# Dropping semaphore waits that another wait implies, in a row-wise absolute maximum

## The chip, the cores and the metric

The kernel runs on one core of one Trainium2 chip. The metric is the device time of one execution in microseconds (us), measured outside the profiler; a profile's "span" leaves out some 2.7 us of it. Executions that are compared ran on the same chip in the same rounds.

## The reference

```python
def setup_inputs():
    return {"x": np.random.randn(8192, 8192).astype(np.float32)}

def reference(x):
    return np.linalg.norm(x, ord=np.inf, axis=1)
```

For a matrix, this norm with `axis=1` is the largest absolute value of each row: 268 MB are read and 32 KB written.

## The kernel before

SyncE (SP) issues every load, and VectorE (DVE) reduces each loaded buffer. There are three buffers of 128 x 16384 numbers in turn (8.4 MB each). Twenty-four bulk loads fill whole buffers; the rest of the matrix comes in pieces that get smaller, so that little is left to reduce when the last piece lands.

```python
    sbuf = ctx.enter_context(tc.tile_pool(name="sbuf", bufs=BUFS))     # BUFS = 3
    ...
    def absmax(o, i):
        return nc.vector.reduce_max(out=o, in_=i, axis=X, apply_absolute_value=True)

    for a in range(A):
        for n in range(G):
            t = sbuf.tile([P, W + PAD], F32, tag="t")
            nc.sync.dma_start(out=t[:, :W], in_=x_b[a, n])             # 24 bulk loads
            absmax(r_bulk[:, a, n * B : (n + 1) * B], ...)
    for i, loads in enumerate(TAIL):                                   # 7 tiles, 21 loads
        ...
    # the last tile: 13 loads, each reduced as it lands, then the last store
    nc.sync.dma_start(out=out_t, in_=r_tail[:])
```

A load into a used buffer has two reasons to wait. The buffer's previous load must have landed (a semaphore of one of eight "lanes", raised by the DMA engines), and the reduction of that data must be over (one counter, raised by VectorE). As this program is built, a load or a reduction carries at most one wait itself; its other waits stand in wait-only instructions (`EVENT_SEMAPHORE` in the profile) ahead of it, one or two in each. As built, a bulk load is this pair:

```text
SP EventSemaphore  waits lane 0 >= 16        the earlier load of this buffer has landed
SP DMACopy         waits DVE    >= 2         its reduction is over; then issue
```

The first wait says nothing new: the reduction itself waited for that landing.

## Time and profile before

| quantity | value | from |
|---|---|---|
| time | 627.62 us median of 6 (627.34 to 628.16) | runs beside the changed kernel |
| span | 624.7 us | page |
| rate in the bulk | 434 GB/s, 19.33 us a load | windows |
| issue to landing of a bulk load | 40.7 us median | line of the load |
| one bulk reduction | 17.22 us | groups |
| fetches of instructions during the span | 2, of 8 KB each | queue 14 |

Two lines of the view of SyncE's waits show what the prediction rests on (who waits, for whom: us in total, times, longest us).

```profile
SPq L187 <- DVE r_bulk L180: 361.6, 21, 17.2
SPq L187 <- DMA t<-in_x_dram: 54.8, 21, 20.1
```

SyncE waits twice for each of the 21 bulk loads, and the wait for VectorE is the one that ends last, after 17.2 us.

```profile
q14 instruction: 2, 0.02, 0.0%
```

### The profile page before, as it was taken

The page shows a single profiled execution, that of the slowest core. Times are in us where ns is not written, and L with a number is a line of the kernel's source. Part 1 is how long each engine was busy: PE and PEld are TensorE (multiplying, and loading weights), DVE is VectorE, ACT ScalarE, POOL GpSimd, SP SyncE. Part 2 cuts the span into 40 slices and gives each one's busy share as a digit, 9 for nine tenths or more (in the row PEclk, how much of TensorE's full clock was granted, in tenths as well). Part 3 has the DMA queues.
Part 4 walks back from the last instruction along what each step waited for, and adds up shares of the span by engine and source line. Part 5 has one row for each costly group of instructions (what it writes and reads, how often), then busy time and mean ns, then how long its engine had stood idle before and what let it go on. Part 6 is the DMA issues. An engine that isn't in the chain of part 4 may idle for free.

```text
span 624.7 us, 189 instructions
## 1 busy us (share of the span) xinstructions
DVE 553.0 (89%) x67; POOL 0.2 (0%) x4
## 2 busy tenths in 40 slices
DVE  0588988889988889888898888988889999999999
POOL 0000000000000000000000000000000000000000
DMA  9999999999999999999999999999999999999998
GB/s 403 462 411 453 420 449 424 432 441 403 470 403 470 403 470 403 453 420 453 420 441 432 424 449 403 470 403 470 403 438 425 445 417 443 421 427 432 423 423 342
DMA packets 9138, 268.48 MB, mean 430 GB/s; under 512 B 1712, under 2 KB 1712, under 8 KB 3248
## 3 DMA queue, kind: packets, MB, share of 16 engines
q1 hardware_dynamic: 8352, 268.44, 99.6%
q10 hardware_dynamic: 784, 0.02, 0.1%
q14 instruction: 2, 0.02, 0.0%
HBM read 268.44 MB, written 0.03 MB: 430 GB/s over the span
## 4 chain that ended last, share of the span: by engine, by line
DMA 67%; DVE 31%; issue 1%; another core or an unknown queue 0%; DVEq 0%; SPq 0%
DMA t<-in_x_dram 67%; DVE r_bulk L180 24%; DVE part L180 6%; DVE t L180 2%; DVEq L270 0%; DVE r_tail L180 0%; SPq L199 0%
## 5 line engine op out<-in xcount | busy, mean ns | idle before, releaser
L180 DVE TENSOR_REDUCE r_bulk<-t 128x2 f32<-128x16384 f32 x24 | 413.3, 17220 | 69.7 <-DMA t<-in_x_dram 69.7
L180 DVE TENSOR_REDUCE part<-t 128x1 f32<-128x8192 f32 (+20 forms) x28 | 121.5, 4411 | 0.3 <-DMA t<-in_x_dram 0.3
L180 DVE TENSOR_REDUCE t<-t 128x1 f32<-128x1664 f32 (+8 forms) x11 | 16.7, 1577 | 0.1
L180 DVE TENSOR_REDUCE r_tail<-t 128x1 f32<-128x644 f32 (+1 forms) x2 | 1.6, 818 | 0.0
L177 DVE MEMSET part<- 128x56 f32 x1 | 0.1, 105 | 0.9 <-PEq L259 0.9
L180 DVE TENSOR_REDUCE r_tail<-part 128x14 f32<-128x56 f32 x1 | 0.2, 202 | 0.0
L259 POOL MEMSET const-bfloat16-1.0<- 128x1 bf16 x1 | 0.1, 103 | 0.0
L259 POOL MEMSET const-uint8-127<- 128x1 uint8 x1 | 0.1, 102 | 0.0
L259 POOL MEMSET const-float32-0.0<- 128x1 f32 x1 | 0.1, 100 | 0.2 <-issue 0.2
L259 POOL MEMSET const-float32-1.0<- 128x1 f32 x1 | 0.1, 99 | 0.0
## 6 DMA issues: line engine op xcount, KB each, us to landing
t<-in_x_dram SPq DMA_DIRECT2D x2, 3392.0 KB, 37.2
t<-in_x_dram SPq DMA_DIRECT2D x1, 5376.0 KB, 40.5
t<-in_x_dram SPq DMA_DIRECT2D x1, 4864.0 KB, 32.9
t<-in_x_dram SPq DMA_DIRECT2D x1, 4800.0 KB, 32.8
t<-in_x_dram SPq DMA_DIRECT2D x1, 4672.0 KB, 34.7
t<-in_x_dram SPq DMA_DIRECT2D x3, 1536.0 KB, 36.9
t<-in_x_dram SPq DMA_DIRECT2D x1, 3520.0 KB, 42.7
t<-in_x_dram SPq DMA_DIRECT2D x1, 3328.0 KB, 40.4
```

The source lines that it names most:

```text
L177: nc.vector.memset(part[:], 0.0)
L180: return nc.vector.reduce_max(out=o, in_=i, axis=X, apply_absolute_value=True)
L259: nc = _bacc.Bacc("TRN2", target_bir_lowering=False, num_devices=1)
```

## The change

When the program is finalized, a pass walks through it. It notes which lane values VectorE must have seen by each value of its counter. A lane wait of a load or store on SyncE is dropped where the VectorE value that the same instruction waits for implies it. On VectorE, a wait for its own counter is dropped where the load whose landing is waited for was itself issued behind that value. Twenty-nine wait-only instructions on SyncE and two on VectorE disappear; nothing is added or reordered. The core of the diff:

```diff
+def drop_implied_waits(nc):
+    ...
+        if type(i).__name__ == "InstDMACopy":
+            ...
+            if i.engine == sp and own and len(waits) > 1:
+                known = upto[own - 1]
+                insts[n] = rewait(i, [s for s in waits
+                    if s.id == counter or s.wait_value > known.get(s.id, 0)])
+        elif i.engine == dve and own and len(waits) > 1:
+            past = max(behind.get((s.id, s.wait_value), 0) for s in waits)
+            if past >= own:
+                insts[n] = rewait(i, [s for s in waits if s.id != counter])
     ...
+    nc.at_finalize(drop_implied_waits)
     nc.at_finalize(start_first_load_early)
```

(Lines are joined here; cuts are marked with dots.)

## The prediction

> **What bounds the kernel now.** I read the page first (busy shares, slices, queues), then the windows, then the order of time in the stream and at the end. The page of the kernel before says that the transfers are never idle; VectorE (DVE) is the only computing engine that does anything to speak of:
>
> ```profile
> span 624.7 us, 189 instructions
> DVE 553.0 (89%) x67; POOL 0.2 (0%) x4
> DMA  9999999999999999999999999999999999999998
> DMA packets 9138, 268.48 MB, mean 430 GB/s; under 512 B 1712, under 2 KB 1712, under 8 KB 3248
> ```
>
> The reader is to see the row of nines: there is no slice in which the 16 DMA engines stand still. The view by windows gives the rate in a stretch of the bulk, in which three loads of 8.389 MB (128 partitions x 16384 numbers of 4 bytes) pass, and in the last part (columns: window, its length, DVE busy, POOL busy, clock, DMA share, GB/s):
>
> ```profile
> 136.00:194.00 58.00, 51.66 (x3) 0.00 (x0) 1.00 1.00 434
> 600.00:612.00 12.00, 11.99 (x7) 0.00 (x0) 1.00 1.01 424
> ```
>
> Three loads in 58.00 us are 19.33 us a load. One bulk reduction takes 17.22 us, so DVE waits about 2.1 us for each load; in the last 150 us it works without a gap, level with the transfers. 268.44 MB at 434 GB/s are 618.5 us. About 6.2 us of the 624.7 us span are the start, the slightly slower small loads and the finish. So the kernel is bound by transfer rate, and a removed instruction can help only where it makes a transfer start earlier into an empty queue, or shortens the last few microseconds.
>
> How full is the queue? The time line of the bulk shows the DMA issues on the queue of SyncE (SP) among the reductions (start, length, what):
>
> ```profile
> 21.99 17.22 DVE L180 TENSOR_REDUCE r_bulk<-t 128x2 f32<-128x16384 f32 x1 [21.01 <-DMA t<-in_x_dram]
> 39.23 0.33 SPq L187 DMA_DIRECT2D t<-in_x_dram  x1
> 41.27 17.22 DVE L180 TENSOR_REDUCE r_bulk<-t 128x2 f32<-128x16384 f32 x1 [2.06 <-DMA t<-in_x_dram]
> ```
>
> The reduction ends at 39.21 and the next load is issued at 39.23, and then takes 40.8 us to land by the view of the bulk load's line, where moving it takes only 19.33 us. The difference, 21.4 us, is time in line behind the load before it: an issue may come that much late, or early, and the rate stays the same.
>
> **What the Trainium skill says.** (1) "DMA: Bandwidth & Descriptors", section "Anatomy of one DMA — SWDGE (gpsimd) path": a wait for a semaphore is made by the issuing sequencer before it dispatches; the DMA engines only drain their queues. This trace agrees for SP: its queue holds, and the engines go on at 434 GB/s. (2) Same page, "Where 436 GB/s comes from": 16 ports give 435.2 GB/s. The 434 GB/s of the window agrees, so there is no spare rate for the change to find. (3) "Perfetto Trace Analysis", section "Identifying Dependency Chains": an instruction with several waits may have EventSemaphore instructions put before it that carry the others. This is what the diff removes, and the trace shows them, 17 ns each on SP. (4) "VectorE: DVE Perf Modes", section "The DRAIN you can't avoid": chained operations took the same time with a semaphore after each as with one after the last. Here too, waits that are already met cost no visible gap: in the last part consecutive reductions with waits begin about 0.08 us before the recorded end of the one in front.
>
> **The change, part by part.** The order of the instructions shows nothing added and nothing moved: 29 SP and 2 DVE wait instructions go, while all loads, reductions and stores keep their order and sizes. The rows of the removed waits on SP, by line, and the one ahead of the last store:
>
> ```profile
> L187 SPq EVENT_SEMAPHORE  x21: 17/17/17, 22.0 to 408.7; - x21
> L199 SPq EVENT_SEMAPHORE  x7: 17/17/28, 428.0 to 544.3; - x7
> L242 SPq EVENT_SEMAPHORE  x1: 17/17/17, 617.0 to 617.0; - x1
> ```
>
> *Part 1, SP bulk, 21 instructions.* Each waits for the landing of the load three back, and the load that follows it then waits for the reduction of that same buffer. The landing comes first: the first removed wait is met at 22.0 and the load goes out at 39.23, when the reduction has ended. So 21 x 17 ns = 0.36 us are spent while SP would be waiting some 17 us each time anyway. On the path: 0.
>
> *Part 2, SP tail, 7 instructions.* As long as 28 ns where one waits on two semaphores, at most 7 x 28 = 0.20 us together. The same order holds: the last one is met at 544.3 and the load behind it is issued at 553.29, when the reduction is over. On the path: 0. Even if each cost its full time on the issue, 0.02 to 0.03 us stand against the 21 us for which the load waits in line.
>
> *Part 3, the last store, 1 instruction.* Met at 617.0; the store goes out at 623.97, after the last reduction. On the path: 0.
>
> *Part 4, DVE, 2 instructions of 21 ns.* The first is met at 478.2, while the last bulk reduction runs until 483.90, and the next starts at 483.82, already overlapping it: 0. The second stands ahead of the first reduction of the last tile, and here the trace shows something that can be gained:
>
> ```profile
> 603.20 2.41 DVE L180 TENSOR_REDUCE part<-t 128x1 f32<-128x2176 f32 x1
> 605.54 0.33 SPq L224 DMA_DIRECT2D t<-in_x_dram  x1
> 605.61 2.42 DVE L180 TENSOR_REDUCE t<-t 128x1 f32<-128x2176 f32 x1
> ```
>
> The load issued at 605.54 waits on the same semaphore as that reduction, so the landing is known by 605.54. The reduction starts at 605.61, at the recorded end of the one before, instead of the usual 0.08 us ahead of it. Without the extra instruction it could start about 0.06 us earlier (about 605.55). But three reductions later DVE has to wait for data again:
>
> ```profile
> 610.26 3.89 DVE L180 TENSOR_REDUCE t<-t 128x1 f32<-128x1664 f32 x2
> 612.25 0.33 SPq L224 DMA_DIRECT2D t<-in_x_dram  x1
> 612.24 0.02 issue
> 612.26 9.90 DVE t L180 x8
> 622.16 0.23 issue
> 622.39 0.59 DVE r_tail L180
> ```
>
> The first two lines are the time line, the others the chain that ended last. The 1664-wide reduction of 1.88 us that began at 610.26 ended at 612.14; the next began only at 612.26, when its load had landed (612.24). From there DVE runs back to back to its end at 623.94. So the 0.06 us won at 605.61 becomes 0.06 us more of waiting at 612.14. On the path: 0.
>
> The two extra waits ahead of the final two reductions stay in both kernels. Sum of the parts on the path: 0 us, with an upper estimate of 0.06 us if the landing at 612.24 also came earlier. All removed time added up, 0.36 + 0.20 + 0.02 + 0.04 = 0.62 us, is an upper limit that assumes everything serial, and it is 0.1% of 627.4.
>
> **The rivals.** *(a) SP issues sooner, and the transfers gain.* If the split wait delayed each of the 28 loads, the change would save up to 28 x 17 to 28 ns, about 0.5 to 0.6 us, giving some 626.8. For it: the waits are ahead of each load on an in-order queue. Against it: each is met microseconds before the wait that releases the load, and 21 us of queue stand in between. *(b) The removed wait has a substitute.* SP would now hold at the load itself on DVE's semaphore. If a DMA instruction that holds longer woke more slowly than one that follows a fresh wait, each issue would be later; the present lag from the reduction's end to the issue is only about 0.02 us, and the line of two loads hides any likely growth. Time: 627.4. *(c) The order of the small loads shifts.* Earlier issues might change how loads share the engines in the tail, and with it the landing at 612.24, which sets the end. Tail issues after the first of the last tile are tied to landings, whose waits stay, so I expect shifts of some 0.1 us, of either sign. *(d) VectorE is the bound at the end,* so two instructions there shorten it by 0.04 to 0.06 us: the 0.12 us gap ahead of 612.26 speaks against it, and it would not be visible in the time in any case.
>
> **Range and chances.** The prediction is the median of before, 627.4, with 0 taken off. The three runs of before spread over 0.8 us (627.34 to 628.16), larger than every term above. The low end allows rival (a) in full, 626.8; the high end is the highest run of before. That gives 626.8 to 628.2. A change of 2% is 12.5 us: no sum of these waits comes within a factor of 20 of it, nor can the rate exceed the limit it is at. Faster by over 2%: 0.005; slower by over 2%: 0.01, for a disturbed chip; within 2%: 0.985.
>
> **What would show it right or wrong.** In the profile of the changed kernel: 158 instead of 189 instructions; the DMA row still all nines and 434 GB/s in the bulk window; each bulk load still about 40.7 us from issue to landing; each issue still some 0.02 us behind the end of a reduction; the first reduction of the last tile 0.05 us or so earlier against the end of the one before; a gap ahead of the second 1664-wide reduction grown by as much; and the end again some 12.4 us after that landing. I am wrong if the loads' rate or the lag from reduction to issue has changed, or the median is outside the range.

## The result, and the profile after

The changed kernel takes 627.50 us (median of 6, 627.38 to 627.97), the kernel before 627.62 us. The ratio is 0.9999 with a 95% interval of 0.9986 to 1.0012. Ratios here are the mean time of one kernel's runs over that of the other's of the same rounds, so they are not quite the ratio of the quoted medians. Nothing changed within what these runs can resolve, and 627.50 lies in the predicted range.

The page of the changed kernel, line by line as shown of before:

```profile
span 624.8 us, 158 instructions
DVE 552.8 (88%) x67; POOL 0.2 (0%) x4
DMA  9999999999999999999999999999999999999998
q14 instruction: 1, 0.01, 0.0%
```

There are 31 instructions less, the transfers are as busy as before, and one fetch of instructions is gone. The windows (length, DVE, POOL, clock, DMA share, GB/s) have the same rates:

```profile
136.00:194.00 58.00, 51.66 (x3) 0.00 (x0) 1.00 1.00 434
600.00:612.00 12.00, 12.00 (x7) 0.00 (x0) 1.00 1.01 424
```

The time line of the bulk, and SyncE's waits for its loads:

```profile
21.98 17.22 DVE L236 TENSOR_REDUCE r_bulk<-t 128x2 f32<-128x16384 f32 x1 [21.01 <-DMA t<-in_x_dram]
39.22 0.33 SPq L243 DMA_DIRECT2D t<-in_x_dram  x1
...
SPq L243 <- DVE r_bulk L236: 417.2, 21, 37.4
```

The load is issued 0.03 us behind the end of the reduction, as before. SyncE's total wait for these loads is the same: 361.6 + 54.8 = 416.4 us in two rows before, 417.2 us in one row now. The wait instruction is gone, the waiting is not.

The start of the last tile, where VectorE's second dropped wait stood:

```profile
603.63 2.41 DVE L236 TENSOR_REDUCE part<-t 128x1 f32<-128x2176 f32 x1
605.95 0.33 SPq L280 DMA_DIRECT2D t<-in_x_dram  x1
605.95 2.42 DVE L236 TENSOR_REDUCE t<-t 128x1 f32<-128x2176 f32 x1
```

The reduction at 605.95 now begins 0.08 us before the recorded end of the one ahead (603.63 + 2.41 = 606.04), together with the load that waits for the same landing; before, it began at that end. So the dropped wait did free some 0.08 us there, and the span did not get shorter. But everything in these lines is some 0.4 us later than before (603.20, 605.54 and 605.61). The experiments show where that comes from.

### The profile page after: what moved, and what is told of

It is laid out like the page before. It is cut to its first block, busy times and chain, and to the rows that moved or that the text cites. A ratio compares the mean times of both kernels' runs of the same rounds, so it can differ in the third digit from the quotient of the medians.

```text
span 624.8 us, 158 instructions
## 1 busy us (share of the span) xinstructions
DVE 552.8 (88%) x67; POOL 0.2 (0%) x4
## 4 chain that ended last, share of the span: by engine, by line
DMA 63%; DVE 36%; another core or an unknown queue 0%; issue 0%
DMA t<-in_x_dram 63%; DVE r_bulk L236 25%; DVE part L236 8%; DVE t L236 3%; DVE r_tail L236 0%
```

## The experiments

All are built on the kernel before, unless said, and all gave the right result. Where wait instructions are added, each as built carries two waits that are already met.

**Theory:** every removed wait was met well before the wait that sets the issue, the loads stand in line ahead of the DMA engines, and so neither part of the change is on the path. **Rivals:** a wait costs its time on an in-order queue; VectorE sets the end; something else that goes with fewer instructions acts.

### Each part alone

```diff
# e1_sp_only: the change without its part for VectorE
-        elif i.engine == dve and own and len(waits) > 1:
+        elif False:
# e2_dve_only: the change without its part for SyncE
-            if i.engine == sp and own and len(waits) > 1:
+            if False:
```

> Only the 29 waits on SyncE are dropped, the two on VectorE stay. Theory (every removed wait on SyncE was met microseconds before the wait that releases the load): 0.0 us against the kernel before, so 627.4 to 627.6 with the spread of the runs. Rival (each wait costs its time on an in-order queue in front of a transfer): 29 x 17 to 28 ns less, 0.5 to 0.8 us. In the profile the two VectorE waits (21 ns each) are still there, and the first reduction of the last tile again starts at the end of the one before it or later, not 0.08 us ahead of it, if its data come as late as before.

> Only the two waits on VectorE are dropped, the 29 on SyncE stay. Theory: the first reduction of the last tile starts up to 0.08 us ahead of the recorded end of the one before it, as all others do; the end of the kernel does not move by more than 0.1 us, because VectorE waits for a landing three reductions later or because the landings themselves shift by more than that: ratio 1.000. Rival (VectorE is the bound of the end): 0.04 to 0.08 us less, which the interval could not show; the profile decides it.

Measured: SyncE's part alone 627.72 us, ratio 1.0004 (0.9991 to 1.0017); VectorE's part alone 627.53 us, ratio 1.0001 (0.9988 to 1.0015); the kernel before 627.57 us. Neither part changes the time, so two effects do not cancel at the scale of the intervals, which is 0.13% or 0.8 us. These times alone do not exclude the 0.5 to 0.8 us of the rival for SyncE: the interval of that part reaches down to 0.9991, or 0.6 us less. The unchanged lag from reduction to issue and the experiments below speak against it. With VectorE's waits kept, the wait and the reduction start 0.06 us apart again (605.48 and 605.54); without them, the reduction starts 0.08 us ahead of the recorded end before it (606.00).

### The suspected cost on SyncE, thirty times larger

```diff
# e3_sp_30_before: at each of the 30 loads and stores with a split wait
+            out += [only_wait(nc, i.engine, lanes[:1]) for _ in range(60)]   # built as 30 instructions
```

> The kernel before with the suspected cost made thirty times larger: 30 further wait instructions, each met already, in front of every load that has the split wait and in front of the last store (900 more on SyncE), at the place of the wait that the change removes. At 17 ns recorded each they take 0.5 us or more at each of the 30 places, 15 us or more together. Theory: SyncE executes them while it would be waiting for VectorE anyway, so the time stays 627.4 to 627.7 (ratio 1.000). The one place that may show: the first load of the last tile, where the landing is met last, is issued 0.5 us later, which its line of loads hides. Rival (cost in series): 15 us more, ratio 1.024.

Measured: 632.05 us against 627.57, ratio 1.0073 (1.0060 to 1.0086). This is a miss: 4.5 us more where the theory said none and the rival 15. The next lines are from three views of this kernel: the line of the bulk load (count: shortest, median, longest ns), the time line, and the queues.

```profile
L247 SPq EVENT_SEMAPHORE  x21: 28/28/28, 23.7 to 413.4; - x21
...
21.93 17.22 DVE L240 TENSOR_REDUCE r_bulk<-t 128x2 f32<-128x16384 f32 x1 [20.96 <-DMA t<-in_x_dram]
39.17 0.33 SPq L247 DMA_DIRECT2D t<-in_x_dram  x1
...
q14 instruction: 9, 0.07, 0.0%
```

The added instructions have no source line and are not listed in these views; the wait in the first line is the last of the 31 at each load. The load landed at 21.90, and the last of the 31 wait instructions started at 23.74. They therefore run some 0.06 us apart, twice and more of what is recorded as their length, and take 1.9 us together. Still the load goes out at 39.17, 0.02 us behind the end of the reduction, so SyncE's time is hidden as the theory says. In the last tile, the same waits delay one issue (584.24 instead of an estimated 582.4); a delay was expected there, but of 0.5 us and not 1.8. What is new is the third line: nine fetches of instructions instead of two. The chain of waits shows where the time goes (start, length, what):

```profile
253.41 40.74 DMA t<-in_x_dram
...
311.42 41.44 DMA t<-in_x_dram
```

The time from issue to landing is 40.74 us for one load. It is 41.44 us for the load issued at 311.42, which stood in line behind loads that were held up after a fetch at 300.9. Over the bulk the landings keep the 19.3 us pace and then step back, by 0.7 us after each of the fetches at 220.4, 300.9, 376.6 and 454.6, and by less after those at 66.9 and 142.4. The landing of the last bulk load comes at 470.33 instead of 466.66.

The records of single transfers in the packed trace show how. Each bulk load ends with 16 records of 4 bytes, by this reading one for each of the 16 DMA engines' shares, and it lands 0.3 to 0.5 us after the last of them. For the last bulk load these lie within 0.76 us in the kernel before. Here 15 of them lie within 1.10 us, and one comes 4.50 us after the first. So one share falls back by some 0.7 us at a time, the load has to wait for it, and the others go on as before. So the cost belongs to the fetched instructions, not to the waiting.

### The issue itself made late

```diff
# e4_sp_10_on_path: ten drains between the release of the buffer and the load, at 29 loads
+            out.append(drain(nc, i.engine, waits))
+            out += [drain(nc, i.engine, []) for _ in range(9)]
+            i = rewait(i, [])
# e7_sp_10_store: the same, ahead of the last store alone
```

> The kernel before with ten sequencer-only instructions (drains, 0.12 us recorded each) between the release of the buffer and the load, at all 29 loads that have the split wait; the last store is left as it is. Now the issue itself is late, by an estimated 1.2 to 2 us at each load. Theory: the lag from the end of a reduction to the issue grows from 0.02 to 1.2 to 2 us, the time from issue to landing falls from 40.7 by as much, and the rate stays 434 GB/s in the bulk window: 627.4 to 628 us. Rival (a late issue costs its lateness): 29 x 1.2 to 2 us, 35 to 58 us more.

> The kernel before with the same ten drains on SyncE between the last reduction and the last store, at this one place alone. Theory: the issue of the store is on the path that sets the end, so the time grows by the full length of the ten, an estimated 1.2 to 2 us (the same length as the lag that each load gets where they stand in front of the loads). Rival (SyncE's own work never shows): no change.

Measured: with the drains ahead of the 29 loads 628.56 us against 627.57, ratio 1.0018 (1.0006 to 1.0031); ahead of the last store alone 627.86 against 627.44, ratio 1.0007 (0.9995 to 1.0020). The size was misjudged: ten drains add 0.53 us, not 1.2 to 2. Only the rise with the loads is clear of the noise. In the time line, the load that was issued at 39.23 goes out later, and VectorE's next reduction stays:

```profile
22.04 17.22 DVE L242 TENSOR_REDUCE r_bulk<-t 128x2 f32<-128x16384 f32 x1 [21.07 <-DMA t<-in_x_dram]
39.81 0.33 SPq L249 DMA_DIRECT2D t<-in_x_dram  x1
41.32 17.22 DVE L242 TENSOR_REDUCE r_bulk<-t 128x2 f32<-128x16384 f32 x1 [2.06 <-DMA t<-in_x_dram]
```

The lag behind the reduction is 0.56 us in the median of the bulk loads, and the median time from issue to landing falls from 40.7 to 40.2. In series this would be 29 x 0.53 = 15 us; 1.0 us came, and it came with fetches. The landings stay within 0.1 us of the kernel before until 350.7 and then step back by 0.7 us twice, behind fetches at 352.6 and 541.4; a fetch at 161.1 left no step. Ahead of the last store, the same ten drains put the store 0.56 us behind the last reduction instead of 0.03, as the theory says of a place on the path; the time moved by 0.4 us, but the interval holds 1, so the profile alone shows that the place is on the path.

### VectorE: the same waits at two places

```diff
# e5_dve_80_first, e6_dve_80_second: 80 met wait instructions behind the first or second dropped wait
+            if n == 1:      # or n == 2
+                out += [only_wait(nc, i.engine, lanes) for _ in range(160)]
```

> The kernel before with 80 further wait instructions, all met, on VectorE behind the first of its two removed waits (the first reduction of the tail). Each is 21 ns as recorded, so 1.7 us or more; if the spacing of such instructions is nearer to 60 ns it is up to 4.8 us. Theory: the landing is met at 478.2 and the engine is busy with the last bulk reduction until 483.9, which leaves 5.7 us for them: no change of the time, and no gap in front of that reduction. Rival (wait instructions on VectorE cost their time wherever they stand): 1.7 to 4.8 us more.

> The same 80 wait instructions behind the second of the two removed waits (the first reduction of the last tile), which is met only 0.06 us before the engine falls idle. Theory: they stand in the open, the reduction starts 1.7 to 4.8 us later, VectorE has no slack left but the 0.1 us at 612.1, and the end moves by 1.6 to 4.7 us. This is the control: it shows that a wait instruction does cost time where it stands on the path. Rival (the end is set by the landings, and VectorE can catch up): no change.

Measured: first place 629.23 us, ratio 1.0030 (1.0018 to 1.0043); second place 635.40 us, ratio 1.0130 (1.0116 to 1.0143); the kernel before 627.44 us. The time lines of the two kernels, with the idle time of VectorE in brackets:

```profile
486.94 8.69 DVE L227 TENSOR_REDUCE part<-t 128x1 f32<-128x8192 f32 x1 [2.59 <-issue]
...
613.90 2.42 DVE L227 TENSOR_REDUCE t<-t 128x1 f32<-128x2176 f32 x1 [8.19 <-issue]
```

Eighty instructions took some 8.2 us at either place, 0.10 us each, where the estimate was 0.02 to 0.06. At the second place all of it became idle time (8.19 us) and the time grew by 8.0 us: VectorE has practically no slack in the last 20 us. At the first place the landing came at 478.62 in this run and the last bulk reduction ended at 484.35. That hides 5.7 us; the rest, 8.3 - 5.7 = 2.6 us, is the 2.59 us of idle time, of which 1.8 us (by the medians) reached the end. The expectation of no change was wrong because the waits were larger than the spare time, but the spare time is what the theory said. A single met wait at the first place lies within 5.7 us and costs nothing.

### How late may an issue be?

```diff
# e8_one_later, e9_two_later: the 21 bulk loads wait for a later reduction
+    copy.replace(s, wait_value=s.wait_value + 1)      # or + 2
```

> The kernel before, with each of the 21 bulk loads that wait for a reduction waiting for the next reduction instead, so each is issued 19.3 us later. Theory: the line of 21.4 us ahead of each load covers this with some 2 us to spare, so the time from issue to landing falls from 40.7 to 21.4 us and the time hardly changes; as a first load on an empty queue took 22.0 us to land where moving it takes 19.3, the spare 2 us may be short by up to 0.6 us a load, so 0 to 13 us more. Rival (a late issue costs its lateness): 21 x 19.3, over 400 us more.

> As the run with one reduction later, but two reductions later: each bulk load is issued only when VectorE has finished with every load before it. That is 38.7 us late, more than the line of 21.4 us. Theory: now the queue runs empty; a load costs 22.0 us to land after its issue and 17.2 us of reduction, 39.2 us instead of 19.33, so 21 x 19.9 = 417 us more, some 1045 us. If the time stayed near 627 us, the reading that the line of waiting loads is what hides late issues would be wrong.

Measured: one later 652.08 us, ratio 1.0398 (1.0382 to 1.0414), 24.6 us more, or 1.2 us for each of the 21 loads that are issued 19.3 us or more later; two later 1044.5 us (one run), 417 us more, as computed. The median time from issue to landing, from the parts on DMA issues of the two kernels in this order:

```profile
t<-in_x_dram SPq DMA_DIRECT2D x24, 24.2
...
t<-in_x_dram SPq DMA_DIRECT2D x24, 21.9
```

A load on an empty queue takes 21.9 us to land, not 19.33, so of the 40.7 us at most 40.7 - 21.9 = 18.8 us are time in line. A delay of 19.3 us exceeds this by 0.5 us. The measured cost is more than twice that, and why is left open. For the change it does not matter: by this estimate an issue has some 18 us to spare, and the removed waits are 0.06 us each.

### Chance, or the fetch of instructions?

> The kernel before, unchanged, profiled a second time, to see how much the landings in the tail move without any change. In the first profiles the load that landed at 583.19 in the kernel before landed at 583.67 in the changed one, although both were issued within 0.01 us of the same time. Theory: that difference is chance, so it can fall on either side here, and the end of the span moves by up to 0.6 us with it. Rival: it belongs to the changed kernel, and this landing is at 583.2 again.

> The changed kernel profiled a second time. Theory: the landing at 583.67 of its first profile is chance and may be at 583.2 or elsewhere here; the first reduction of the last tile starts about 0.08 us ahead of the end of the one before it again; time 627.4 to 628.0. Rival: the late landing belongs to the change, and is at 583.7 again.

Measured: the kernel before 627.68 us and the changed one 627.25 us, one run each. The landing in question came at 583.62 and 583.50, which alone would fit chance: whole stretches of landings lie some 0.4 us later in one profile than in another. The intervals between landings leave such shifts out, and for them the theory of chance fell. The records of the DMA queues show at what time instructions are fetched, and two intervals between landings move with them:

| kernel | fetches of 8 KB at (us) | landing of the 4352-wide load after the one before it | landing of the second 1664-wide load after the one before it |
|---|---|---|---|
| before, first and second profile | 592.0, 609.4; 592.4, 609.7 | 5.20; 5.20 | 2.24; 2.26 |
| SyncE's part alone | 609.4 | 5.19 | 2.36 |
| VectorE's part alone | 582.2, 592.5 | 5.57 | 1.99 |
| changed, first and second profile | 582.2; 582.0 | 5.68; 5.34 | 1.98; 1.98 |

The first interval is 5.19 or 5.20 us in all eleven profiles without a fetch at 582, those of the other experiments included. SyncE's dropped waits take away the fetch near 592. VectorE's two dropped waits move a fetch from 609 to 582. The load in flight at 582 then lands 0.14 to 0.48 us later, and the one in flight at 609 some 0.3 us earlier. The later landing is the 0.4 us by which the last tile began late in the profile of the changed kernel. (In four other kernels, those with 30 waits, with drains at the loads, with one reduction later and with 900 drains on TensorE, a fetch at this place leaves the second interval at 1.93 to 1.98 us. In each of them at least one of the shares named above was already a microsecond or more behind most others.) The time between the first and the last landing was 600.97 and 601.19 us before, and 601.15 and 600.78 after, so no gain or loss remains that these profiles can show. That the later landing at 582 and the earlier one at 609 nearly cancel was not foreseen, and is luck. Why two instructions less move a fetch by 27 us was not settled.

```diff
# e12_pe_900: 900 drains on TensorE, which has no work in this kernel
+    body.instructions = [mybir.InstDrain(..., engine=mybir.EngineType.PE, ...)
+        for _ in range(900)] + list(body.instructions)
```

> The kernel before with 900 drains on the queue of TensorE, which has nothing to do in this kernel and which nothing waits for before the end. It tells apart why the 900 waits on SyncE cost 4.5 us where 0 was expected. Theory now: it is not SyncE's time, but the fetching of the longer program: that run's trace has 9 transfers of instructions of 8 KB each where the kernel before has 2, and the landings there step back by some 0.73 us after each. Then 900 instructions on an idle engine cost about as much: 7 more fetches, all in the first 100 us, and 2 us (7 x 0.31 us, the recorded length of one) to 5 us (7 x 0.73) more in all. Rival (SyncE's own time in front of the loads is the cost): no more fetches that matter, 0.0 us, because no load is issued later than before.

Measured: 628.40 us against 627.45, ratio 1.0013 (0.9999 to 1.0027). The size is below what was expected, and the interval just holds 1. The profile tells more. The first line is from its queues, the other two from its chain of waits:

```profile
q8 instruction: 3, 0.05, 0.0%
...
0.79 41.94 DMA t<-in_x_dram
42.73 0.02 issue
```

TensorE's instructions came in three fetches of 16 KB on a queue of their own, the first at 19.2 us. The second load landed at 42.73 where the kernel before has 41.24 (first load: 23.42 against 21.96). One fetch of twice the size thus cost 1.46 us, twice 0.73. The following landings keep that distance of 1.4 to 1.5 us up to the last tile (1.0 to 1.1 us at the end), so the other two fetches added nothing. The last records of the shares show why: the first fetch puts one of the 16 behind, the second and the third one more each, and from the third load on three come 1.9 to 2.2 us after the first and the other 13 within 0.9 us. The three are late side by side, and a load waits only for the last. The fetch at 161.1 that left no step in the kernel with drains at the loads moved a share that was not the last: the last record came 0.83 us after the first before it and 0.85 after it. SyncE did nothing more in this kernel, and the loads landed later all the same. So more instructions can delay transfers without any queue being held up by them.

## Why the prediction was right

**The bound.** It held: 434 GB/s in the bulk window, and no idle slice of the DMA row, before and after. (The section that the prediction cites for 435.2 GB/s also has a lower figure for reads from HBM, which the prediction left out; see the last section.)

**Parts 1 and 2, SyncE's loads.** They held. The lag from reduction to issue is 0.03 us in both kernels, and each bulk load still takes 40.7 us to land. That nothing is gained is shown by this lag, by thirty times the waits (no later issue in the bulk), and by a lag of 0.56 us at the loads (1.0 us instead of 15); the time of the part alone (1.0004) agrees, but its interval is too wide to show it. Two terms were mis-sized. A wait-only instruction on SyncE occupies it for about 0.06 us, not for the recorded 0.017 to 0.028 us, so the limit with everything in series is about 29 x 0.06 = 1.8 us instead of 0.56, and a change of 2% is some 7 times as much, not 20. Some 0.065 us lie between the start of a wait with one semaphore and the load behind it (578.006 and 578.071 in the kernel before). The time in line is at most 18.8 us, not 21.4, since a load on an empty queue takes 21.9 us.

**Part 3, the last store.** It held: the store follows the last reduction by 0.03 us in both kernels. Ten drains at this place did delay it, so the place is on the path, but the removed wait was met 7 us earlier.

**Part 4, VectorE.** The reduction in the last tile starts 0.08 us earlier against the one before it, as predicted from the trace. A wait-only instruction is visible there, with 0.065 us from its start to that of the reduction (recorded: 21 ns), so "no visible gap" in point (4) of the prediction holds only for waits that a reduction carries itself. The next step of the argument failed in the profile taken: the gap of 0.12 us ahead of the second 1664-wide reduction did not grow, it vanished (610.60 to 612.48, and the next reduction at 612.39). VectorE came to that point late, because its data had landed late behind the moved fetch. The conclusion, no gain at the end, stands for another reason than the one given.

**The rivals.** Rival (a), earlier issues, and rival (b), a slower wake-up, are refuted by the unchanged lag; e4 shows besides that an issue 0.5 us later costs nothing like 0.5 us. Rival (c), shifted landings of some 0.1 us of either sign, came nearest to what happened: they shift by 0.1 to 0.5 us, but through fetches of instructions, which the prediction did not consider. Rival (d) had half the truth: VectorE has almost no slack at the end (8.0 us of 8.2 came through), yet 0.08 us is beneath what can be seen.

## What to carry to other kernels

Before counting what a wait instruction costs, look at which wait ends last at that place, and how much work stands in line behind it: here 29 waits were all met 7 to 17 us early, 21 of them ahead of bulk loads with an estimated 18 us in line, and dropping them gained nothing that could be seen. Waits implied by others can pay off only in the open, as on an engine that is about to run dry. In a kernel bound by transfers, also read the row of instruction fetches: blocks of instructions travel through the same DMA engines, a load lands with the last of its 16 shares, and a change of a few instructions can move such a block.

## What the Trainium skill lacked or had wrong

- "Runtime: NRT & Kernel Launch", "Instruction fetch mechanics", says that engines refill their instructions in blocks of 16 KiB and that crossing a block is "mostly hidden". Here TensorE's blocks are 16 KB, but those on queue 14, which come and go with instructions of SyncE and VectorE, are 8 KB. In a kernel that keeps the DMA engines full they are not always hidden: where the fetch falls on the share of a load that comes last, the landings step back by some 0.73 us for 8 KB, and once by 1.46 us for 16 KB, though an 8 KB fetch is recorded with only 0.31 us. Where it falls on another share, the step is smaller or none.
- "DMA: Bandwidth & Descriptors", "Queues, rings and completion order", names refills of the runtime on row 14 and says that the engines take the rows in turn, but not what such a packet costs a load beside it: 0.14 to 0.48 us in the tail here.
- The section that the prediction cites, "DMA: Bandwidth & Descriptors", "Where 436 GB/s comes from", also says that for transfers between HBM and SBUF the HBM side binds at about 358 GB/s. The 434 GB/s measured here from HBM, with one core running, are above that, and the measurement decides.
- No page gives the time of a wait-only instruction whose semaphores are already met. With one wait it takes 0.065 us on SyncE and on VectorE (recorded: 17 and 21 ns), seen at one place each. With two waits it takes 0.06 us on SyncE (recorded: 28 ns) and 0.10 us on VectorE (recorded: 50 ns). A drain on SyncE is recorded with 0.12 us, but ten in a row added 0.53 us.
